# Norm scalings on the activation engine, earlier norm weights, modulation tiles in four column groups, urgent level products: one change to a two-layer backbone kernel

## The chip, the cores and the metric

One core of one Trainium2 chip runs the kernel. The metric is the device time of one execution in microseconds (us), the median of three runs. The core has five engines with a queue each, which run beside each other and wait for each other by semaphores: PE (TensorE: matmuls, and PEld, its weight loads), DVE (VectorE), ACT (ScalarE), POOL (GpSimd) and SP (SyncE, which issues most of the DMAs). An engine works its queue in order.

## The reference, cut to what matters

A backbone of two layers on 512 latent tokens and 256 context tokens, width 1024. Each layer takes six modulation vectors from a conditioning vector (one for latents, one for the context), mixes, and runs a convolution FFN. The mixer of layer 0 has four gated linear-attention heads and a chunk MLP; that of layer 1 has multi-head latent attention with six heads and a Fourier mix. The change touches these parts:

```python
# modulation: 6 x 1024 values for the latents and for the context
mod_l = (silu_c @ ada_w[l] + ada_b[l])[:, None, :]
mod_c = (silu_cc @ ada_w[l] + ada_b[l])[None, None, :]
# layer 0: gated linear attention, one head; readout norm
o = rms_norm(o.transpose(0, 2, 1, 3), onorm_w) * silu(g)
# layer 0: chunk MLP, the "gate values" v are normalised per token and group of 128
u = gelu(u_pre)
v = rms_norm(gelu(v_pre).reshape(bsz, n, 128, 4, 128), vnorm_w)
y = u * (einsum('gts,bnsgc->bntgc', ws, v) + bs.T[:, :, None])
# layer 1: queries and keys are normalised per token and head, rotary part apart
q_nope = rms_norm(q[..., :128], qn_w[:128])
q_pe   = rope_2d(rms_norm(q[..., 128:], qn_w[128:]), cos, sin)
k_pe   = rope_2d(rms_norm(p[..., 640:], kn_w[128:]), cos, sin)
scores = softmax(q @ k.T * 192 ** -0.5)
```

## The kernel before, in words

Everything stays in float32; a product of two matrices is made as three matmuls of high and low parts (`mm3`, L505 to L510). For the weights, `split` (L485) makes the high part `wh` with a cast on ACT (L486) and the low part `wl` with a subtraction, `raw - wh`, on POOL for the kinds in `on_pool` (L498 for a whole 128x1024 chunk, L490 in two halves for the kinds in `by_half`, L495 for other forms of the same). A scheduler of the language orders every engine's queue when the program is built; `high_priority(200)` raises the instructions under it, and pools of tiles (name and number of buffers) decide when a tile may be written again. Weight and modulation loads are issued on SP's queue, some small tables on ACT's.

**Modulation** (`ada_group`, L567). Two layers with three groups each, of 16 half tiles of 128x1024. The conditioning vector stands as a stationary operand of 32 columns (`sc_pad`); a half tile is the moving operand of two matmuls of 512 columns (L577), which land in two of the four groups of 32 PSUM partitions; the other half tile of the same k goes to the other two. Generators in the queue `bg["ada"]` are advanced between other matmuls. At the end of a group the sums are copied (`asb`, L585), transposed (L589) and added to the bias (L594). Layer 0's later groups run under the head projections; layer 1's second group fills the gap between its projections and attention, its third runs in attention.

**GLA heads** (`gla`, a generator in `bg["gla"]` that `tick` advances between projection matmuls). For each of seven levels: block matmuls on PE (L827, or L855 from level 5) from Q products in `qk` and K products merged into `scr`; the result is written into `near` under a mask (L848); then DVE multiplies Q by decay factors (L868), K (L870) and the factors themselves (L872), and ACT copies the K products into `scr` (L835) for the next level. Each of L868 and L870 is one 128x768 multiplication. The tail of a head: squares on ACT (L923), a reciprocal root by Newton steps on DVE (`rsqrt`, L460 to L465, eleven tiny instructions), the scaling into `scr` (L930), transposes on PE (L939), and the products that end in the output slot (L940, L943 on ACT, L944 on POOL).

**Chunk MLP** (L977 to L1021). The gate values `vp` (six token chunks, 512 columns in four groups of 128) get a gelu, squares and a rsqrt `mr` of 24 columns. POOL scales `vp` by `mr` in six 128x512 multiplications (L997). Then `drain("gla")` runs what is left of the last head (its tail), and four groups follow, each with a projection, a gelu, matmuls that have `vp` as the stationary operand (L1011) and products.

**Layer 1, before attention.** The query latents `qt` get squares, `rstd`, a scaling (L1450) and are transposed and split into `lt` (`turn_q`, L1456, ACT L1347, DVE L1348). The table `pewb` of norm weights for the rotary part is fetched by a DMA on ACT's queue (L1433), behind it the rope table (L1435). The rotary keys are scaled with it (L1464), rotated (`rope`, L1364 to L1369) and the table itself is scaled (L1470); this block stands ahead of the call that projects the keys (`keys(0, ...)`, with L1611 and L1613 on ACT, L1614 on DVE). Then keys are scaled (L1622, two on DVE and one on POOL), values projected, and `fill` puts modulation matmuls between.

**Queries** (`scale_queries`, L1568). For each of three pairs of heads, DVE scales the rotary part (L1571) and POOL the rest, in two 128x512 multiplications (L1574). Scores (L1730), maxima on DVE (L1733 to L1735), exponentials on ACT (L1738) and transposes (L1749) follow.

## Time and profile before

| what | value |
|---|---|
| median of three runs | 1649.61 us (1648.12 to 1650.98) |
| the profiled execution's own time | 1649.35 us |
| its span, first to last instruction | 1647.6 us |
| PE busy | 1591.9 us, 97% of the span |
| DVE, ACT, POOL busy | 1140.8, 703.4, 649.1 us |
| mean granted TensorE clock | 0.992 |

The span is 1.75 us shorter than the time; what lies around it is the start and end of the launch. A busy share is an average: where PE is idle, the row of the instruction that follows names in square brackets how long its engine stood idle and what ended that. A granted clock of 1.00 is 2.4 GHz, 0.50 is 1.2 GHz.

### The profile page before, as it was taken

The numbers are of one execution on the slowest core, as the hardware profiler recorded it, in microseconds if no ns is written. First come the engines' busy times: TensorE is split into PE (matmuls) and PEld (weight loads), VectorE is DVE, ScalarE is ACT, GpSimd is POOL, SyncE is SP. The second block draws the span as 40 slices with busy tenths as digits, with TensorE's granted clock in tenths as the row PEclk, the third lists the DMA queues.
The fourth block names the chain that finished last, engine by engine and source line by source line (L and its number), as shares of the span: only waits on it lengthen the run. The fifth ranks groups of instructions, "written<-read, shape, count | busy, mean of one in ns | idle before, by whom it ended". The sixth has DMA issues, their size and how long they took to land.

```text
span 1647.6 us, 28314 instructions
## 1 busy us (share of the span) xinstructions
PE 1591.9 (97%) x11206; PEld 1420.5 (86%) x11206; DVE 1140.8 (69%) x2134; ACT 703.4 (43%) x1328; POOL 649.1 (39%) x421
## 2 busy tenths in 40 slices
PE   8999999989999999999999999898899899999998
PEld 7777777678989999999999989676799898999997
DVE  5447675753565666676666775767874799999984
ACT  4323333523444333233332444465665555555551
POOL 1221223344625566565665513331208322323321
PEclk9999999999999999999999999999999999999999
DMA  9453434333412121222212322752105223223222
GB/s 355 159 187 116 142 116 137 120 102 103 130 50 64 61 80 55 74 77 62 80 55 75 90 68 82 250 171 93 52 27 167 90 85 108 103 90 116 103 78 77
DMA packets 53205, 175.11 MB, mean 106 GB/s; under 512 B 5712, under 2 KB 7760, under 8 KB 53072
## 3 DMA queue, kind: packets, MB, share of 16 engines
q1 hardware_dynamic: 51632, 170.66, 31.1%
q10 hardware_dynamic: 1440, 2.64, 0.4%
q8 instruction: 88, 1.44, 0.3%
q14 instruction: 45, 0.37, 0.1%
HBM read 171.18 MB, written 2.10 MB: 105 GB/s over the span
## 4 chain that ended last, share of the span: by engine, by line
PE 79%; DVE 14%; ACT 2%; DMA 2%; issue 2%; POOL 1%; DVEq 0%; SPq 0%; ACTq 0%; POOLq 0%
PE mm L508 17%; PE mm L510 16%; PE mm L509 16%; PE aux L508 7%; PE aux L509 7%; PE aux L510 7%; PE aux L577 2%; DVE qk L870 1%; DVE qk L868 1%; DVE wp L387 1%; PE aux L1143 1%; PE mm L1730 1%; DMA x<-in_xt_dram 1%; DMA raw<-in_w_dram 1%; PE aux L1749 1%
## 5 line engine op out<-in xcount | busy, mean ns | idle before, releaser
L498 POOL TENSOR_TENSOR wl<-raw,wh 128x1024 fp32r<-128x1024 f32 (+5 forms) x100 | 210.2, 2104 | 356.6 <-ACT wh L486 304.5
L486 ACT CAST wh<-raw 128x1024 fp32r<-128x1024 f32 (+5 forms) x155 | 146.5, 947 | 141.0 <-PE mm L509 63.8
L387 POOL TENSOR_TENSOR wp<-sum,wp 128x512 fp32r<-128x512 f32 x80 | 115.9, 1454 | 163.4 <-ACT wp L385 153.9
L508 PE MATMUL mm<-xt,wh 128*128 128x256 f32 (+1 forms) x384 | 135.1, 353 | 0.9 <-ACT xt L648 0.9
L510 PE MATMUL mm<-xt,wl 128*128 128x512 f32 (+1 forms) x384 | 129.4, 338 | 0.0
L509 PE MATMUL mm<-xt,wh 128*128 128x512 f32 (+1 forms) x384 | 129.3, 337 | 0.0
L509 PE MATMUL mm<-slot,wh 128*128 128x512 f32 (+1 forms) x336 | 113.4, 338 | 1.0 <-POOL slot L1253 0.7
L508 PE MATMUL mm<-slot,wh 128*128 128x512 f32 (+1 forms) x336 | 113.5, 339 | 1.0 <-ACT slot L1252 1.0
L510 PE MATMUL mm<-slot,wl 128*128 128x512 f32 (+1 forms) x336 | 113.1, 337 | 0.0
L385 ACT CAST wp<-sum 128x512 fp32r<-128x512 f32 x100 | 60.8, 620 | 122.2 <-PE aux L509 61.5
L1028 DVE SCALAR_TENSOR_TENSOR xl<-mm,mods,xl 128x512 f32<-128x512 f32 (+1 forms) x84 | 58.5, 696 | 70.7 <-PE mm L510 70.2
L495 POOL TENSOR_TENSOR wl<-raw,wh 128x512 fp32r<-128x512 f32 (+2 forms) x50 | 55.7, 1135 | 129.1 <-ACT wh L486 123.6
L387 POOL TENSOR_TENSOR wp<-raw,wp 128x512 fp32r<-128x512 f32 x60 | 80.0, 1341 | 52.3 <-ACT wp L385 52.3
L385 ACT CAST wp<-raw 128x512 fp32r<-128x512 f32 x100 | 62.1, 621 | 78.5 <-DMA raw<-in_w_dram 27.7
L508 PEld LDWEIGHTS mm<-xt,wh 128*128 128x128 f32 x384 | 72.0, 188 | 27.0 <-issue 16.8
L508 PE MATMUL mm<-kt,wp 128*128 128x256 f32 x320 | 90.4, 282 | 3.8 <-ACT t L1216 3.8
L490 POOL TENSOR_TENSOR wl<-raw,wh 128x512 fp32r<-128x512 f32 x22 | 35.7, 1622 | 138.0 <-DVE t L1245 92.3
L510 PE MATMUL mm<-kt,wp 128*128 128x256 f32 x320 | 89.8, 281 | 0.0
L509 PE MATMUL mm<-kt,wp 128*128 128x256 f32 x320 | 89.7, 280 | 0.0
L510 PEld LDWEIGHTS mm<-xt,wl 128*128 128x128 f32 x384 | 72.3, 188 | 8.2
L509 PEld LDWEIGHTS mm<-xt,wh 128*128 128x128 f32 x384 | 72.2, 188 | 8.3
L509 PE MATMUL mm<-lt,wh 128*128 128x256 f32 (+2 forms) x236 | 78.1, 331 | 1.2 <-DVE lt L1253 1.2
(390 smaller groups left out, 5272.7 us busy)
## 6 DMA issues: line engine op xcount, KB each, us to landing
raw<-in_w_dram SPq DMA_DIRECT2D x162, 512.0 KB, 3.5
ada_t<-in_ada_dram SPq DMA_DIRECT2D x80, 512.0 KB, 4.4
raw<-in_w_dram SPq DMA_DIRECT2D x31, 384.0 KB, 3.1
wp<-in_w_dram SPq DMA_DIRECT2D x20, 512.0 KB, 4.4
kt<-in_ada_dram SPq DMA_DIRECT2D x16, 512.0 KB, 7.0
raw<-in_w_dram SPq DMA_DIRECT2D x10, 256.0 KB, 2.6
xl<-in_xt_dram SPq DMA_DIRECT2D x2, 1024.0 KB, 8.0
out_dram<-xl SPq DMA_DIRECT2D x8, 256.0 KB, 2.0
```

The source lines that it names most:

```text
L385: S.copy(h, a)
L387: e.tensor_tensor(l, a, h.bitcast(F32), op=ALU.subtract)
L486: S.copy(h, raw)
L490: e.tensor_tensor(l[:, c], raw[:, c], h[:, c].bitcast(F32), op=ALU.subtract)
L495: G.tensor_tensor(l[:, c], raw[:, c], h[:, c].bitcast(F32), op=ALU.subtract)
L498: e.tensor_tensor(l, raw, h.bitcast(F32), op=ALU.subtract)
L508: T.matmul(ps, a[0], b[0], start=first, stop=False, **kw)
L509: T.matmul(ps, a[0], b[1], start=False, stop=False, **kw)
L510: T.matmul(ps, a[1], b[0], start=False, stop=last, **kw)
L577: T.matmul(ps[32 * q:32 * q + 32, :], sc_pad[:, k, :], t[:, j * 512:(j + 1) * 512], start=(k == 0), stop=(k == KD - 1))
L868: V.tensor_tensor(qa, qa, pick(FF[:], NT + m, [[2 * m, nb], [-(NT + m), 2], [0, m]]), op=ALU.mult)
L1028: V.scalar_tensor_tensor(xs, ps, gate, xs, op0=ALU.mult, op1=ALU.add)
```

## The change

Seven edits, with the lines of the kernel before. (1) `split`: for the kinds of layer 0 that begin with `ev_` the subtraction on POOL is made as two halves of 512 columns. (2) `ada_group`: a half tile of 1024 columns is the moving operand of four matmuls of 256 columns, one for each group of 32 PSUM partitions, where it was two of 512; the order in which the results are read is changed to match. (3) The two level products L868 and L870 stand under `high_priority(200)`. (4) The last head is run up to its tail before the groups of the chunk MLP, and the tail is run after the first group's projection is issued. (5) The gate values are scaled on ACT, one 128x128 activation for each chunk and group (24 in all, six ahead of each group's projection), where POOL had six multiplications. (6) The table `pewb` lies in a pool that is open from the start; its DMA is written where layer 0's pools close, and since nothing holds it back the scheduler puts it on ACT's queue among the squares of the first norm; the scaling and rotation of the rotary keys moves into `rotate_keys()`, called after the values' projection. (7) `scale_queries`: eight 128x128 activations on ACT for each pair, where POOL had two 128x512 multiplications.

```diff
@@ split
-        if kind[:5] == "down1":
+        if kind[:5] == "down1" or kind[:3] == "ev_" and kind in on_pool:
             n = raw.shape[-1] // 2
-            for e, c in ((G, slice(0, n)), (V, slice(n, 2 * n))):
+            for e, c in ((G, slice(0, n)), (V if kind[:2] == "do" else G, slice(n, 2 * n))):
                 e.tensor_tensor(l[:, c], raw[:, c], h[:, c].bitcast(F32), op=ALU.subtract)
@@ ada_group
-                for j in range(2):
-                    q = 2 * hf + j
-                    T.matmul(ps[32 * q:32 * q + 32, :], sc_pad[:, k, :], t[:, j * 512:(j + 1) * 512],
-                             start=(k == 0), stop=(k == KD - 1))
+                for q in range(4):
+                    T.matmul(ps[32 * q:32 * q + 32, hf * 256:(hf + 1) * 256], sc_pad[:, k, :],
+                             t[:, q * 256:(q + 1) * 256], start=k + hf == 0, stop=k + hf == KD, skip_group_check=True)
@@ gla
             qa = pick(QQ, 0, dd)
-            V.tensor_tensor(qa, qa, ...)
+            with tc.high_priority(200):
+                V.tensor_tensor(qa, qa, ...)
             ka = pick(KK, 0, dd)
-            V.tensor_tensor(ka, ka, ...)
+            with tc.high_priority(200):
+                V.tensor_tensor(ka, ka, ...)
...
-        yield
+        yield "tail"
@@ chunk MLP
-    for c in range(6):
-        a = vp[c // 3][:, c % 3, :].rearrange("p (g d) -> p g d", g=4)
-        G.tensor_tensor(a, a, mr[:, c * 4:c * 4 + 4].unsqueeze(2).to_broadcast([P, 4, P]), op=ALU.mult)
-    drain("gla")
+    while next(bg["gla"][0]) != "tail":
+        pass
     for g in range(4):
+        for c in range(6):
+            a = vp[c // 3][:, c % 3, g * P:(g + 1) * P]
+            S.activation(a, a, AF.Copy, scale=mr[:, c * 4 + g:c * 4 + g + 1])
         ps = proj(("ev_in", 20 + g), X)
+        drain("gla")
@@ layer 1
     l0.close()
     lp = ctx.enter_context(tc.tile_pool(name="l1", bufs=17))
+    pewb = sm.tile([P, 128], F32, tag="pew", name="pewb", bufs=1)
+    nc.scalar.dma_start(pewb[:], pew.to_broadcast([P, 128]))
...
-    pewb = l1c.tile([P, 128], F32, name="pewb")
-    nc.scalar.dma_start(pewb[:], pew.to_broadcast([P, 128]))
...
+    def rotate_keys():
...
     project_v(0)
+    rotate_keys()
     fill(2)
@@ scale_queries
-        q4 = rq.rearrange("p j (g d) -> p j g d", g=2)
-        for j in (slice(0, 2), slice(2, 4)):
-            G.tensor_tensor(q4[:, j], q4[:, j], r[:, j, 0:2].unsqueeze(3).to_broadcast([P, 2, 2, P]), op=ALU.mult)
+        for j in range(4):
+            for g in range(2):
+                q = rq[:, j, g * P:(g + 1) * P]
+                S.activation(q, q, AF.Copy, scale=r[:, j, g:g + 1])
```

Three places where the order of an engine's queue changes:

POOL's queue around the chunk MLP, before and after. In it `wl` is the low part of a weight, `vp` the gate values, `mr` their reciprocal root, `slot` the output of a head (L944; L946 in the change).

```order
L498 TENSOR_TENSOR wl<-raw,wh 128x1024 x9
L997 TENSOR_TENSOR vp<-vp,mr 128x512 x6
L944 TENSOR_TENSOR slot<-slot 128x512
L944 TENSOR_TENSOR slot<-slot 128x256
L498 TENSOR_TENSOR wl<-raw,wh 128x1024
```

```order
L490 TENSOR_TENSOR wl<-raw,wh 128x512 x18
L946 TENSOR_TENSOR slot<-slot 128x512
L946 TENSOR_TENSOR slot<-slot 128x256
L490 TENSOR_TENSOR wl<-raw,wh 128x512 x2
L1025 TENSOR_TENSOR slot<-U,slot 128x512
```

The six multiplications are gone, and POOL has nothing between the last weight and the head's output. On ACT the scalings stand behind the squares of the last head (L925 in the change, L923 before):

```order
L925 ACTIVATE junk,ss<-aux 128x128 x6
L1002 ACTIVATE vp<-vp,mr 128x128 x6
L584 COPY asb<-aux 128x512
L1002 ACTIVATE vp<-vp,mr 128x128 x8
L945 CAST slot<-slot 128x512
L945 CAST slot<-slot 128x256
L1002 ACTIVATE vp<-vp,mr 128x128 x8
L1009 ACTIVATE U<-mm 128x512
L1009 ACTIVATE U<-mm 128x256
L486 CAST wh<-raw 128x1024
L1002 ACTIVATE vp<-vp,mr 128x128 x2
```

So six of the 24 stand ahead of the copy `asb`, and eight ahead of the casts of the head's output.

DVE's queue in the levels of a GLA head, before and after (two levels and the start of a third). L870 is the product of K, L868 that of Q (L872 and L869 in the change, where L872 of before is L874).

```order
L870 TENSOR_TENSOR qk<-qk,slot 128x384x2
L848 COPY_PREDICATED near<-mk,aux 128x192
L868 TENSOR_TENSOR qk<-qk,slot 128x384x2
L872 TENSOR_TENSOR slot<-slot 128x768
L870 TENSOR_TENSOR qk<-qk,slot 128x192x2x2
L848 COPY_PREDICATED near<-mk,aux 128x192
L868 TENSOR_TENSOR qk<-qk,slot 128x192x2x2
L872 TENSOR_TENSOR slot<-slot 128x384
L960 TENSOR_TENSOR slot<-mm,slot 128x512
L960 TENSOR_TENSOR slot<-mm,slot 128x256
L870 TENSOR_TENSOR qk<-qk,slot 128x96x2x4
```

```order
L872 TENSOR_TENSOR qk<-qk,slot 128x384x2
L869 TENSOR_TENSOR qk<-qk,slot 128x384x2
L848 COPY_PREDICATED near<-mk,aux 128x192
L874 TENSOR_TENSOR slot<-slot 128x768
L872 TENSOR_TENSOR qk<-qk,slot 128x192x2x2
L869 TENSOR_TENSOR qk<-qk,slot 128x192x2x2
L848 COPY_PREDICATED near<-mk,aux 128x192
L874 TENSOR_TENSOR slot<-slot 128x384
L962 TENSOR_TENSOR slot<-mm,slot 128x512
L872 TENSOR_TENSOR qk<-qk,slot 128x96x2x4
```

The Q product now follows the K product at once, and the masked copy and the second half of the projection's product stand behind.

DVE's queue in layer 1 where the rotary keys are scaled, before and after; `pewb` is the fetched table, `qt` the query latents, L1348 the low part of the transposed latents that the query projection waits for (in the change L1470 is L1464 of before, L1454 is L1450, L1629 is L1622, L1354 is L1348).

```order
L460 TENSOR_SCALAR rsd<-qs 128x4
L1464 SCALAR_TENSOR_TENSOR kp_9915<-lt,rsd,pewb 128x64
L461 TENSOR_SCALAR rsd<-rsd 128x4
L1464 SCALAR_TENSOR_TENSOR kp_9915<-lt,rsd,pewb 128x64
...
L1470 TENSOR_TENSOR rope_t<-rope_t,pewb 128x512
L465 SCALAR_TENSOR_TENSOR rsd<-rst,rsd 128x4
L1614 TENSOR_REDUCE s_9931<-sq 128x4
L1450 TENSOR_SCALAR qt<-qt,rsd 128x384 x4
...
L1348 SCALAR_TENSOR_TENSOR lt<-aux,vt,lt 128x512
...
L1622 TENSOR_TENSOR lt<-lt,r_9933 128x512 x2
```

```order
L1454 TENSOR_SCALAR qt<-qt,rsd 128x384 x4
L1621 TENSOR_REDUCE s_10078<-sq 128x4 x2
L1350 TENSOR_TENSOR kt<-mm,kt 128x256
L1571 TENSOR_SCALAR s_10078<-s_10078 128x12
L1470 SCALAR_TENSOR_TENSOR kp_10227<-lt,rsd,pewb 128x64
...
L1370 TENSOR_TENSOR lt<-kp_10227,rope_t 128x4x64
L1629 TENSOR_TENSOR lt<-lt,r_10080 128x512 x2
L1375 TENSOR_TENSOR lt<-lt,rope 128x4x2x16 x2
L1476 TENSOR_TENSOR rope_t<-rope_t,pewb 128x512
L1354 SCALAR_TENSOR_TENSOR lt<-aux,vt,lt 128x512 x3
```

The chain of the query latents no longer stands behind the table, but the low parts L1354 (L1348 before) now stand behind the scaled keys and the rotation.

## Rows read from the trace of the kernel before

**Rows 1.** The page's first part: each engine's busy us, share of the span and instructions.

```profile
PE 1591.9 (97%) x11206; PEld 1420.5 (86%) x11206; DVE 1140.8 (69%) x2134; ACT 703.4 (43%) x1328; POOL 649.1 (39%) x421
```

**Rows 2.** Stretches of the span. Columns: the stretch and its length in us; each engine's busy us with the number of instructions; granted clock; share of DMA; GB/s.

```profile
344.28:347.69 3.41, 2.77 (x12) 2.67 (x13) 2.39 (x8) 0.83 (x2) 0.13 (x1) 0.50 0.00 1
1044.01:1047.43 3.42, 3.39 (x16) 2.83 (x20) 3.42 (x8) 2.54 (x7) 1.99 (x2) 0.50 0.02 6
1119.10:1200.00 80.90, 73.72 (x497) 59.98 (x490) 66.90 (x197) 48.88 (x127) 13.34 (x12) 1.00 0.21 72
```

**Rows 3.** The timeline at the last head's tail and the chunk MLP's scaling, DVE, POOL, ACT and PE. Columns: start and duration in us, engine, line, operation, out<-in, shape, count; in brackets the engine's idle time before it and what ended it.

```profile
336.83 0.62 ACT L585 COPY asb<-aux 128x512 f32<-128x512 f32 x1
...
337.01 0.17 DVE L926 TENSOR_SCALAR ss<-ss 128x6 f32<-128x6 f32 x1
337.10 6.03 POOL L997 TENSOR_TENSOR vp<-vp,mr 128x512 f32<-128x512 f32 x6 [2.50 <-DVE mr L465]
...
337.21 0.95 DVE L460 TENSOR_SCALAR rr<-ss 128x6 int32<-128x6 int32 x1
...
342.18 0.96 DVE L463 TENSOR_TENSOR rst<-ss,rr 128x6 f32<-128x6 f32 x1
343.18 0.17 DVE L464 SCALAR_TENSOR_TENSOR rst<-rst,rr 128x6 f32<-128x6 f32 x1
...
344.18 1.02 DVE L930 TENSOR_TENSOR scr<-aux,rr 128x512 f32<-128x512 f32 x2
...
344.92 1.54 PE L939 MATMUL aux<-ct,scr 128*128 128x128 f32 x6 [4.96 <-DVE scr L930]
```

**Rows 4.** Groups of ACT's instructions by line and form: busy us, mean ns of one | idle time before them.

```profile
L1347 ACT ACTIVATE lt<-aux,vt 128x128 fp32r<-128x128 f32 x24 | 8.1, 368 | 5.4 <-PE aux L1590 4.2 <-PE aux L577 0.6 <-DVE lt L1348 0.6
...
L923 ACT ACTIVATE junk<-aux 128x128 f32<-128x128 f32 x24 | 6.3, 278 | 15.1 <-PE aux L918 15.1
```

**Rows 5.** Groups of POOL's instructions by line and form, as in Rows 4.

```profile
L498 POOL TENSOR_TENSOR wl<-raw,wh 128x1024 fp32r<-128x1024 f32 x56 | 135.3, 2416 | 290.2 <-ACT wh L486 273.0 <-PE aux L855 14.3 <-PE aux L827 2.8
...
L495 POOL TENSOR_TENSOR wl<-raw,wh 128x512 fp32r<-128x512 f32 x32 | 41.0, 1303 | 59.7 <-ACT wh L486 57.7 <-issue 1.7 <-DMA raw<-in_w_dram 0.3
```

**Rows 6.** The timeline of two levels of a GLA head, columns as in Rows 3.

```profile
123.49 2.39 POOL L498 TENSOR_TENSOR wl<-raw,wh 128x1024 fp32r<-128x1024 f32 x1 [9.56 <-ACT wh L486]
123.61 3.08 DVE L870 TENSOR_TENSOR qk<-qk,slot 128x768 f32<-128x768 f32 x1
...
126.61 0.36 DVE L848 COPY_PREDICATED near<-mk,aux 128x192 f32<-128x192 uint8 x1
...
126.88 0.94 DVE L868 TENSOR_TENSOR qk<-qk,slot 128x768 f32<-128x768 f32 x1
...
127.97 0.60 PE L827 MATMUL aux<-qk,scr 128*32 128x32 f32 x47 [1.52 <-DVE qk L868]
```

**Rows 7.** L827's matmuls as a group over the whole span: busy us, mean ns of one | PE's idle time before them, and what ended it.

```profile
L827 PE MATMUL aux<-qk,scr 128*32 128x32 f32 x960 | 12.9, 202 | 7.4 <-DVE qk L868 5.2 <-ACT scr L835 2.2
```

**Rows 8.** The timeline of PE, a burst of modulation matmuls that holds both half tiles of a pair (layer 0).

```profile
100.18 1.07 PE L577 MATMUL aux<-ada_t,sc_pad 128*32 128x512 f32 x8
```

**Rows 9.** The same in layer 1, first a burst of three half tiles, then one half tile alone.

```profile
1072.85 1.91 PE L577 MATMUL aux<-kt,sc_pad 128*32 128x512 f32 x12
...
1075.17 1.05 PE L577 MATMUL aux<-kt,sc_pad 128*32 128x512 f32 x4
```

**Rows 10.** L577 alone in stretches: busy us of PE and of PEld (records; two for each instruction), granted clock, share of DMA, GB/s.

```profile
120.00:130.00 10.00, 2.10 (x8) 0.32 (x8) 1.00 0.36 111
208.00:214.00 6.00, 2.10 (x8) 0.29 (x8) 1.00 0.29 87
1052.50:1077.00 24.50, 10.34 (x48) 1.55 (x48) 1.00 0.72 263
1117.00:1175.00 58.00, 9.36 (x40) 1.35 (x40) 0.98 0.29 100
```

**Rows 11.** L577's weight loads: duration in ns, min/median/max, and the starts of the first and the last.

```profile
L577 PEld LDWEIGHTS aux<-ada_t,sc_pad x256: 106/109/154, 70.2 to 1173.0; 128*32 128x32 f32 x128
```

**Rows 12.** The 48 records of a level's block matmuls (L827) on PE.

```profile
122.54 0.63 PE L827 MATMUL aux<-qk,scr 128*32 128x32 f32 x48
```

**Rows 13.** The timeline in layer 1 from the arrival of the table to the query projection, columns as in Rows 3.

```profile
1039.76 0.28 DVE L1464 SCALAR_TENSOR_TENSOR kp<-lt,rsd,pewb 128x64 f32<-128x64 f32 x1 [4.22 <-DMA pewb<-in_pew_dram]
...
1044.04 0.58 PE L508 MATMUL mm<-wh,lt 128*128 128x256 f32 x1 [3.70 <-ACT sq L1613]
...
1045.53 2.15 DVE L1450 TENSOR_SCALAR qt<-qt,rsd 128x384 f32<-128x384 f32 x4
...
1051.43 0.75 DVE L1348 SCALAR_TENSOR_TENSOR lt<-aux,vt,lt 128x512 fp32r<-128x512 f32 x1
...
1052.23 0.44 PE L510 MATMUL mm<-wh,lt 128*128 128x384 f32 x1 [0.22 <-DVE lt L1348]
...
1054.18 2.14 DVE L1622 TENSOR_TENSOR lt<-lt,r 128x512 f32<-128x512 f32 x2
```

**Rows 14.** The timeline in attention, columns as in Rows 3.

```profile
1164.61 0.47 ACT L1738 ACTIVATE pr<-mm,mx 128x256 f32<-128x256 f32 x1 [1.15 <-DVE mx L1735]
...
1165.22 0.39 PE L508 MATMUL mm<-kt,lt 128*128 128x256 f32 x1 [1.12 <-ACT pr L1738]
...
1167.01 2.49 POOL L1574 TENSOR_TENSOR lt<-lt,r 128x512 f32<-128x512 f32 x2 [3.68 <-DVE mx L1740]
```

More of the change, by code (lines that the diff above doesn't have):

```diff
@@ L589, in ada_group @@
             T.transpose(pt[:, b * P:(b + 1) * P], asb[:, b * P:(b + 1) * P], ident)
-        o = mods[l][:, g * 16:(g + 1) * 16, :].rearrange("p (j b) c -> p b j c", b=4)
+        o = mods[l][:, g * 16:(g + 1) * 16, :].rearrange("p (f j e) c -> p f e j c", f=2, e=2)
         i0 = pt[:].rearrange("p (b j r) -> p b j r", b=4, r=32)[:, :, :, 0:2]
-        i1 = vcol("ada_b", l * 48 + g * 16, 16).rearrange("p (j b) -> p b j", b=4).unsqueeze(3)
+        i1 = vcol("ada_b", l * 48 + g * 16, 16).rearrange("p (f j e) -> p f e j", f=2, e=2).unsqueeze(4)
         for b in range(4):
-            V.tensor_tensor(o[:, b], i0[:, b], i1[:, b].to_broadcast([P, 4, 2]), op=ALU.add)
+            f, e = divmod(b, 2)
+            V.tensor_tensor(o[:, f, e], i0[:, b], i1[:, f, e].to_broadcast([P, 4, 2]), op=ALU.add)
         yield
@@ L867, in gla @@
             qa = pick(QQ, 0, dd)
-            V.tensor_tensor(qa, qa, pick(FF[:], NT + m, [[2 * m, nb], [-(NT + m), 2], [0, m]]), op=ALU.mult)
+            with tc.high_priority(200):
+                V.tensor_tensor(qa, qa, pick(FF[:], NT + m, [[2 * m, nb], [-(NT + m), 2], [0, m]]), op=ALU.mult)
             ka = pick(KK, 0, dd)
-            V.tensor_tensor(ka, ka, pick(FF[:], m, [[2 * m, nb], [NT - m, 2], [0, m]]), op=ALU.mult)
+            with tc.high_priority(200):
+                V.tensor_tensor(ka, ka, pick(FF[:], m, [[2 * m, nb], [NT - m, 2], [0, m]]), op=ALU.mult)
             ta = pick(FF[:], 0, [[NT, 2], [2 * m, nb]])
@@ L1460, in backbone @@
     kpe = kt()
-    kp0 = tp.tile([P, 6, 64], F32, tag="t2k", name="kp0")
     kp2 = lt(F32)[:].rearrange("p a b -> p (a b)")[:, 0:768].rearrange("p (c g d) -> p c g d", c=6, g=2)
-    for c in range(6):
-        V.scalar_tensor_tensor(kp0[:, c, :], kvr[c][:, 256:320], kr[:, 6 + c:7 + c], pewb[:, 64:128],
-                               op0=ALU.mult, op1=ALU.mult)
-    G.tensor_copy(kp2[:, 0:2, 0, :], kp0[:, 0:2, :])
-    rope(kp2[:, 2:6, 0, :], kp0[:, 2:6, :])
-    t8 = rope_t[:].rearrange("p (n d) -> p n d", d=64)
-    V.tensor_tensor(t8, t8, pewb[:, 0:64].unsqueeze(1).to_broadcast([P, 8, 64]), op=ALU.mult)
-    G.tensor_copy(kp2[:, :, 1, :], kp2[:, :, 0, :])
+    def rotate_keys():
+        kp0 = tp.tile([P, 6, 64], F32, tag="t2k", name="kp0")
+        for c in range(6):
+            V.scalar_tensor_tensor(kp0[:, c, :], kvr[c][:, 256:320], kr[:, 6 + c:7 + c], pewb[:, 64:128],
+                                   op0=ALU.mult, op1=ALU.mult)
+        G.tensor_copy(kp2[:, 0:2, 0, :], kp0[:, 0:2, :])
+        rope(kp2[:, 2:6, 0, :], kp0[:, 2:6, :])
+        t8 = rope_t[:].rearrange("p (n d) -> p n d", d=64)
+        V.tensor_tensor(t8, t8, pewb[:, 0:64].unsqueeze(1).to_broadcast([P, 8, 64]), op=ALU.mult)
+        G.tensor_copy(kp2[:, :, 1, :], kp2[:, :, 0, :])
     A = []
```

## The prediction

> **What bounds the kernel now.** I read the page first. PE is busy for 1591.9 of 1647.6 us [rows 1], so a change that leaves PE's work alone can win at most the 55.7 us in which PE stands idle, and whatever the clock loses after a long idle time. Then I listed PE's idle times by what ended them, and looked up each that this change can reach. The reader is to see three kinds.
>
> First, the last GLA head's tail. PE stands idle 4.96 us before L939, which waits for the scaling L930 on DVE [rows 3]. Ahead of L930 stands the reciprocal root, eleven tiny instructions. While POOL scales the gate values (6.03 us, six instructions), each of DVE's takes 0.95 to 0.96 us, one for one of POOL's; from 343.18, when POOL is done, the same kind takes 0.17. Behind that idle time the granted clock is 0.50, 1.2 GHz, for 3.41 us with 2.77 of them busy on PE [rows 2].
>
> Second, the levels. K's product L870 took 3.08 us where L868 took 0.94, because POOL's 128x1024 subtraction of 2.39 us had begun 0.12 us earlier [rows 6]; PE then waited 1.52 us. All such waits of L827 come to 7.4 us [rows 7].
>
> Third, layer 1. DVE stands 4.22 us for the table `pewb`, and PE 3.70 us behind it, with the clock at 0.50 for 3.42 us after [rows 2, 13].
>
> Where PE does not wait, the modulation matmuls count in full. A burst of a pair of half tiles takes 1.07 us; a half tile alone takes 1.05, as long as two; three take 1.91 [rows 8, 9]. In a pair, four groups of columns run at once, in a single half tile only two.
>
> My sum is made against the profiled execution, 1649.35 us, which is 0.26 below the median of the three runs; I leave that difference aside. About 0.2% (3.3 us) is what a measurement can tell from no change.
>
> **The parts.**
>
> *Gate values to ACT.* POOL has nothing left to do there, so the eleven instructions go at 0.17 with a pitch of 0.20: from 337.21 to 339.4, L930 starts there and its first half is done some 0.6 later, at 340.0, where it now stands done at 344.9. PE's own work lasts to 339.96 (344.92 less 4.96). The idle time falls from 4.96 to some 0.2, and with it goes the half clock, worth half of the 2.77 us: 1.4. Together −6.1. Bounds: −6.4 if nothing is left; −4.5 if the eleven keep 0.3 and the clock still falls for a part. ACT takes 24 instructions of 128x128 at 0.28 to 0.37 us each [rows 4], 6.7 to 8.9 us in all, of which six stand ahead of `asb` (1.7 to 2.2 us, so it ends by 339.7, still ahead of L939). Their cover is ACT's idle time there; if it were gone, the group's vp matmuls would be late.
>
> *Halves on POOL and urgent products.* A half takes about 1.3 us where the whole takes 2.42 [rows 5]. In rows 3 DVE got in exactly one instruction for each of POOL's. By that, L870 waits for the first half only (1.2 less), but L868 behind it waits for the second half; what is left for certain is that L848 (0.36) no longer stands between them [rows 6]. That is −0.37 for each of six waits, and one where K's product starts earlier by a half: −1.0. Sum −3.2. Bounds: −7.4, if every wait goes, and +1.0, if the halves (0.2 us more POOL time each pair) hit products that were free. The value lies nearest to rows 3, which show the alternation.
>
> *Modulation in four groups.* From rows 8 and 9: a pass of 512 columns adds (1.91−1.07)/2 = 0.42 us, and a burst carries 0.23 beside. A pass of 256 adds 0.21, so a half tile alone takes 0.42+0.23 = 0.65 and a pair stays at 1.07. Whole pairs therefore gain nothing; singles gain 0.40. In layer 0 two pairs are split in two bursts each (2.10 us busy each [rows 10]); the first now goes in one burst (−1.0), the second as one and seven instructions (−0.4): −1.4. In layer 1's fill, twelve half tiles take 10.34 us [rows 10]. In the new order they go as five single ones, one burst of three (six passes, 1.49) and one of four (eight passes, 1.91); the first single one falls into a wait (below), so 4 × 0.65 + 1.49 + 1.91 = 6.0. That is −4.3; I take −4.0, bounds −4.5 and −0.5, the last if the half tiles' arrival becomes the bound. In attention 9.36 us [rows 10] become 7.9 by the same count; half of that lies beside other waits, as PE is idle for 7.2 us of the 80.9 after 1119 [rows 2]: −0.7.
>
> The 320 added weight loads cost nothing in this: L827's weights are of the same shape (128 rows, 32 columns, four groups), and 48 of its records with a load each end in 0.63 us [rows 12], so the loads lie beside the running matmuls. The Trainium skill ("TensorE: Matmul & The Clock Gate", Part 3, the mechanism) says that weight loads overlap running matmuls only where the row groups differ, and here all four use all rows. By that rule the loads would stand in the open, and this term would be a loss (the last rival); rows 12 speak against it, in matmuls of 32 columns only.
>
> *Table and rotation.* The wait of 4.22 us goes, and PE's 3.70 with it [rows 13]. But what PE needs next is L510 at 1052.23, which waits for L1348, and L1348 now stands behind two keys' products (2.14), and the rotation. DVE now begins its wait at 1035.54 (1039.76 less 4.22). Without it, ten more instructions of the latents' root at 0.20 and a reduction of some 0.7 bring L1450 to 1038.3, where it now starts at 1045.53: 7.2 earlier. Put between L1450 and L1348 are six products with the table at 0.28, 1.7 together, L1622's 2.14, and the rotation and the scaling of the table, some 2.0 (an estimate, four instructions of the sizes of these rows and a wait for POOL's share): 5.8 later. L1348 thus comes 1.4 earlier. So most of what is won at 1040 is waited out again before 1052, in a new idle time of PE, with perhaps another stretch of half clock. I take −0.7; bounds −3.0 (the added instructions lie in DVE's waits) and +2.5 (the clock falls on busy work). The DMA at the start costs ACT one issue: +0.2.
>
> *Queries to ACT.* POOL's 2.5 us for each pair [rows 14] go. ACT gets 8 × 0.28 to 0.37, 2.2 to 3.0 us, three times; PE waited there 1.12 us on ACT's exponentials, ACT 1.15 on DVE's maxima. I take 0; bounds −1.5 (DVE's freed time) and +4.
>
> Sum: −6.1 −3.2 −1.4 −4.0 −0.7 −0.7 +0.2 = −15.9, so 1649.35 − 15.9 = **1633.5 us**.
>
> **The rivals.**
>
> *The waits move* (0.26). Halves win nothing, as products alternate with the halves, and the fill's winnings are waited out on DVE or on arriving tiles. What stays is the tail (−6.1), layer 0's splits (−1.4) and a bit of the rest (−0.7): 1641.2. For it speaks that DVE is 69% busy [rows 1] and that the low parts now stand behind the keys; against it, that behind 1052 the rows show PE running without a wait on DVE.
>
> *More than forecast* (0.12). All of L827's waits go (−7.4), the table's term is −3.0 and attention gains 2.2 in all: −6.1−7.4−1.4−4.0−3.0−2.2 = −24.1, 1625.3. For it: priority lets the products pass the projection's; against it: rows 3.
>
> *ACT becomes attention's bound* (0.06). Three times 2.2 to 3.0 us stand in front of exponentials that PE waits for, 7.8, and the tail's −6.1 and −1.4 are all else that holds: 1649.6, no change. Against it: ACT is 43% busy [rows 1], and pair 0's lie ahead of attention.
>
> *Weight loads in the open* (0.04), slower. 320 more at 0.109 us [rows 11] are 34.9 us, less the tail, the levels and the table (10.0): 1674. It decides from a burst of a pair of more than 1.07 + 10.0/40 = 1.32 us. The rule of the Trainium skill named above would bring this about; L827's rows are against it.
>
> **How the numbers follow.** Forecast 0.52, the others as given. Faster by over 0.2%: forecast and the first two rivals, 0.90. Within 0.2%: the third, 0.06. Slower: 0.04. The range goes down to 1624.0, past the second rival's value by the 1.4 us by which attention's and layer 0's terms are uncertain, and up to 1644.0, past the first's by 2.8, about what the queries' bound of +4 leaves beside −1.2 of the rest. Left out are the last two rivals (0.10) and as much of the others' edges.
>
> **What would show it.** Right: L460 to L465 at 337 all near 0.17, no idle time of over 1 us before L939, no 0.50 behind it; half tiles alone in 0.65; no wait on `pewb`; an idle time on PE before the query projection that L1348 ends. Wrong: products of levels still at 2.5 us with PE waiting as long; pair bursts over 1.3; PE waits on exponentials that stand behind the query scalings.

## The result and the profile after

The changed kernel takes 1635.2 us, the median of four runs (1633.43 to 1638.72), where the kernel before took 1650.3 beside it (1648.12 to 1653.59): a ratio of 0.991 [0.9886, 0.9933]. The profiled execution took 1633.43 us with a span of 1631.6, so 15.9 us less than the profiled one of before. PE's idle time fell from 55.7 to 47.0 us (span less busy) and its busy time by 7.3. The first part of the page after, columns as in [rows 1]:

```profile
PE 1584.6 (97%) x11526; PEld 1429.8 (88%) x11526; DVE 1128.5 (69%) x2134; ACT 717.2 (44%) x1376; POOL 653.9 (40%) x457
```

Where the time came from shows when the start of the same PE instruction is taken in both traces and subtracted. Worked out so, in us:

| stretch, by the time in before | after less before at its end | gained or lost in it | forecast |
|---|---|---|---|
| start, to 70 | +0.25 | +0.25 | +0.2 |
| levels and layer 0's splits, to 316 | −7.5 | −7.75 | −4.6 |
| tail, to 387 | −14.3 | −6.8 | −6.1 |
| behind layer 0's FFN norm, to 466 | −12.4 | +1.9 | none |
| to the fill, about 1025 | −12.7 | −0.3 | none |
| fill and table, to 1084 | −14.3 | −1.6 | −4.7 |
| attention, to 1287 | −13.2 | +1.1 | −0.7 |
| behind the last norm, to 1292 | −15.1 | −1.9 | none |
| to the end | −16.0 | −0.9 | none |

So the total is as forecast, and four of its terms are not. Each difference is that of one execution against one: at 70, executions of kernels with the same edit 6 stood between 2.0 us earlier and 2.9 us later than before, so the +0.25 of the first line alone says nothing, and only what comes on top within a stretch is read below.

**The tail went as forecast.** The timeline after, columns as in [rows 3]:

```profile
329.56 1.87 ACT L1002 ACTIVATE vp<-vp,mr 128x128 f32<-128x128 f32 x6 [0.22 <-DVE mr L465]
329.64 0.17 DVE L460 TENSOR_SCALAR rr<-ss 128x6 int32<-128x6 int32 x1
...
331.66 0.17 DVE L465 SCALAR_TENSOR_TENSOR rr<-rst,rr 128x6 f32<-128x6 f32 x1
...
331.87 1.02 DVE L932 TENSOR_TENSOR scr<-aux,rr 128x512 f32<-128x512 f32 x2
...
332.61 0.88 PE L941 MATMUL aux<-ct,scr 128*128 128x128 f32 x6 [0.28 <-DVE scr L932]
```

From the root's first instruction to its last, 2.2 us now stand where [rows 3] have 7.1, each at 0.17. PE's idle time is 0.28 instead of 4.96. Windows after, columns as in [rows 2]; the text comes back to the later ones:

```profile
332.00:345.00 13.00, 12.72 (x83) 11.23 (x82) 6.43 (x13) 8.73 (x25) 7.13 (x6) 1.00 0.38 138
448.00:456.00 8.00, 6.53 (x33) 5.83 (x34) 6.89 (x19) 3.38 (x8) 0.00 (x0) 0.79 0.00 0
...
1040.65:1044.50 3.85, 3.85 (x24) 2.19 (x23) 1.21 (x5) 0.77 (x2) 0.00 (x0) 0.57 0.42 142
...
1102.50:1106.50 4.00, 4.00 (x23) 1.92 (x15) 2.70 (x12) 0.42 (x1) 0.00 (x0) 0.57 0.01 4
1275.50:1283.00 7.50, 7.50 (x61) 7.13 (x60) 5.08 (x13) 3.72 (x9) 0.06 (x1) 1.00 0.01 2
```

The first line is the tail: granted clock 1.00, where [rows 2] have 0.50.

**The levels gained more than forecast.** L827 as a group after, which answers to [rows 7]:

```profile
L827 PE MATMUL aux<-qk,scr 128*32 128x32 f32 x960 | 12.9, 202 | 2.8 <-DVE qk L869 1.6 <-ACT scr L835 1.0
```

Its waits fell by 4.6 us. The deepest levels' matmuls, L855, had a wait of their own that the forecast did not count. In before:

```profile
L855 PE MATMUL aux<-qk,scr 128*128 128x128 f32 x96 | 12.2, 276 | 1.2 <-DVE qk L868 1.2
```

It is 0.0 after. Together that is 5.8 of some 6.3 us (7.75 less the splits' 1.4); some 0.7 of the gain lies ahead of the first level, between 70 and 114. Two levels after, columns as in [rows 6]:

```profile
122.49 0.95 DVE L872 TENSOR_TENSOR qk<-qk,slot 128x768 f32<-128x768 f32 x1
122.83 4.16 POOL L490 TENSOR_TENSOR wl<-raw,wh 128x512 fp32r<-128x512 f32 x2 [9.14 <-PE aux L827]
123.36 0.95 DVE L869 TENSOR_TENSOR qk<-qk,slot 128x768 f32<-128x768 f32 x1
124.97 0.60 PE L827 MATMUL aux<-qk,scr 128*32 128x32 f32 x46
...
292.05 3.25 POOL L490 TENSOR_TENSOR wl<-raw,wh 128x512 fp32r<-128x512 f32 x2 [1.77 <-ACT wh L486]
292.27 1.88 DVE L872 TENSOR_TENSOR qk<-qk,slot 128x768 f32<-128x768 f32 x1
...
294.07 2.04 DVE L869 TENSOR_TENSOR qk<-qk,slot 128x768 f32<-128x768 f32 x1
...
296.26 0.62 PE L827 MATMUL aux<-qk,scr 128*32 128x32 f32 x48 [1.41 <-DVE qk L869]
```

The second pair is what was forecast: each product stands behind one half (1.88 and 2.04), and PE waits 1.41. The first pair is what was not: both products keep their 0.95, and it is POOL that is late (two halves in 4.16 instead of some 2.6). PE does not wait.

**The half tiles have the forecast durations.** A whole pair, 16 records in layer 0, and one half tile alone, 8 records in layer 1, which answer to [rows 8] and [rows 9]; and L576 (L577 before) alone in windows, which answer to [rows 10]:

```profile
99.90 1.07 PE L576 MATMUL aux<-ada_t,sc_pad 128*32 128x256 f32 x16
...
1050.48 0.64 PE L576 MATMUL aux<-kt,sc_pad 128*32 128x256 f32 x8
```

```profile
120.00:130.00 10.00, 1.08 (x16) 0.51 (x16) 1.00 0.27 88
205.00:211.00 6.00, 1.68 (x16) 0.54 (x16) 1.00 0.35 116
1036.00:1062.00 26.00, 5.80 (x80) 2.13 (x80) 0.93 0.49 176
1100.00:1160.00 60.00, 8.86 (x80) 2.51 (x80) 0.97 0.26 89
```

The added weight loads lie beside the running matmuls: the pair of 16 takes 1.07 us as the pair of 8 did, so PE has paid nothing for them. Attention's ten half tiles (the last line) take 8.86 us where the forecast had 7.9.

**Layer 1 has another wait instead.** The timeline after, columns as in [rows 13]:

```profile
1035.74 2.12 DVE L1629 TENSOR_TENSOR lt<-lt,r 128x512 f32<-128x512 f32 x2
...
1038.19 0.68 DVE L1476 TENSOR_TENSOR rope_t<-rope_t,pewb 128x512 f32<-128x512 f32 x1
...
1038.79 2.06 DVE L1354 SCALAR_TENSOR_TENSOR lt<-aux,vt,lt 128x512 fp32r<-128x512 f32 x3
...
1039.58 0.44 PE L510 MATMUL mm<-wh,lt 128*128 128x384 f32 x1 [3.24 <-DVE lt L1354]
```

PE's 3.70 on the table is gone, and 3.24 behind the low parts L1354 stands in its place, with a granted clock of 0.57 behind it (the window at 1040.65). The difference stood at −12.7 us where the fill begins and at −18.2 at 1049 of before; L510 starts at 1039.58 instead of 1052.23, which is −12.65. So the 5.5 us won by then were waited out there, and what the stretch keeps is won behind it. Ahead of L510 stand two of the fill's twelve half tiles (at 1033.03 and 1035.15); the other ten stand behind it.

**Attention lost.** The timeline at the first scores, columns as in [rows 14]:

```profile
1097.65 2.45 ACT L1581 ACTIVATE lt<-lt,r 128x128 f32<-128x128 f32 x8 [2.66 <-DVE r L465]
...
1100.48 0.46 ACT L1746 ACTIVATE pr<-mm,mx 128x256 f32<-128x256 f32 x1
...
1101.08 0.38 PE L508 MATMUL mm<-kt,lt 128*128 128x256 f32 x1 [2.74 <-ACT pr L1746]
```

PE waits 2.74 us for an exponential that stands behind the eight new scalings, and then runs at 0.57 (the window at 1102.5).

### The profile page after: what moved, and what is told of

It is laid out like the page before. It is cut to its first block, busy times and chain, and to the rows that moved or that the text cites. A ratio compares the mean times of both kernels' runs of the same rounds, so it can differ in the third digit from the quotient of the medians.

```text
span 1631.6 us, 29062 instructions
## 1 busy us (share of the span) xinstructions
PE 1584.6 (97%) x11526; PEld 1429.8 (88%) x11526; DVE 1128.5 (69%) x2134; ACT 717.2 (44%) x1376; POOL 653.9 (40%) x457
## 3 DMA queue, kind: packets, MB, share of 16 engines
q10 hardware_dynamic: 1440, 2.64, 0.4%
## 4 chain that ended last, share of the span: by engine, by line
PE 81%; DVE 12%; ACT 3%; issue 2%; DMA 1%; POOL 1%; SPq 0%; ACTq 0%; DVEq 0%; POOLq 0%
PE mm L508 17%; PE mm L510 17%; PE mm L509 17%; PE aux L508 7%; PE aux L509 7%; PE aux L510 7%; PE aux L576 2%; DVE wp L387 1%; PE aux L1147 1%; DVE qk L872 1%; DVE qk L869 1%; PE mm L1738 1%; DMA raw<-in_w_dram 1%; PE aux L855 1%; PE aux L1757 1%
## 5 line engine op out<-in xcount | busy, mean ns | idle before, releaser
L490 POOL TENSOR_TENSOR wl<-raw,wh 128x512 fp32r<-128x512 f32 x118 | 171.1, 1468 | 367.4 <-ACT wh L486 203.5
L498 POOL TENSOR_TENSOR wl<-raw,wh 128x768 fp32r<-128x768 f32 (+6 forms) x52 | 94.2, 1813 | 115.3 <-ACT wh L486 87.7
L509 PE MATMUL mm<-xt,wh 128*128 128x512 f32 (+1 forms) x384 | 130.0, 339 | 0.0
L510 PE MATMUL mm<-xt,wl 128*128 128x512 f32 (+1 forms) x384 | 129.7, 338 | 0.0
L509 PE MATMUL mm<-slot,wh 128*128 128x512 f32 (+1 forms) x336 | 113.4, 337 | 0.7 <-POOL slot L1257 0.7
L510 PE MATMUL mm<-slot,wl 128*128 128x512 f32 (+1 forms) x336 | 113.3, 338 | 0.0
L510 PE MATMUL mm<-kt,wp 128*128 128x256 f32 x320 | 89.8, 280 | 0.0
L509 PE MATMUL mm<-kt,wp 128*128 128x256 f32 x320 | 89.7, 280 | 0.0
L509 PEld LDWEIGHTS mm<-xt,wh 128*128 128x128 f32 x384 | 72.8, 190 | 8.2
L510 PEld LDWEIGHTS mm<-xt,wl 128*128 128x128 f32 x384 | 72.8, 190 | 8.1
L509 PE MATMUL mm<-lt,wh 128*128 128x256 f32 (+2 forms) x236 | 78.5, 333 | 1.2 <-DVE lt L1257 1.2
```

What stands on the lines that cost most here:

```text
L490: e.tensor_tensor(l[:, c], raw[:, c], h[:, c].bitcast(F32), op=ALU.subtract)
L498: e.tensor_tensor(l, raw, h.bitcast(F32), op=ALU.subtract)
L509: T.matmul(ps, a[0], b[1], start=False, stop=False, **kw)
L510: T.matmul(ps, a[1], b[0], start=False, stop=last, **kw)
```

## The experiments

Theory A: the tail, the levels and the table gain as their waits fall; the fill's gain is waited out behind L1354, and the queries on ACT cost attention some 3 us. Its rivals, one for each run: that the tail's gain came from another edit; that halves, not urgency, carry the levels; that the four groups gained in place; and that the queries' cost lies elsewhere.

### The tail by itself

**Edits 4 and 5 put into the kernel before.**

```diff
-        yield
+        yield "tail"
...
-    for c in range(6):
...
-        G.tensor_tensor(a, a, mr[...], op=ALU.mult)
-    drain("gla")
+    while next(bg["gla"][0]) != "tail":
+        pass
     for g in range(4):
+        for c in range(6):
...
+            S.activation(a, a, AF.Copy, scale=mr[...])
         ps = proj(("ev_in", 20 + g), X)
+        drain("gla")
```

> The kernel before with only the gate values moved: 24 activations on ACT, the last head run up to its tail first. Theory (POOL's six multiplications slow DVE's eleven tiny instructions, one for one): these go at 0.17 us, the idle time of 4.96 us before the head's last transposes goes and the half clock behind it with it, 6 us at the end of the tail and at the end: 1644. Rival (the tail waits for the statistics or for ACT, and the earlier run of the tail is what counts): the tiny instructions stay near 0.95 us, or the idle time moves to another wait; less than 3 us.

Measured: 1642.32 us, 0.9951 [0.9937, 0.9964]. The timeline at the tail, columns as in [rows 3]:

```profile
338.23 0.17 DVE L460 TENSOR_SCALAR rr<-ss 128x6 int32<-128x6 int32 x1
...
341.18 0.87 PE L939 MATMUL aux<-ct,scr 128*128 128x128 f32 x6 [0.21 <-DVE scr L930]
```

The root's instructions take 0.17 and PE waits 0.21. By the trace it gains 6.0 us between 338 and 387, and 5.4 are left at the end; by the medians it is 7.8 (5.9 to 10.4), and the profiled execution was the slowest of its five. So the tail's term is shown by itself, and it is the largest of the forecast. What edit 4 gives without edit 5 no run shows.

### The levels: halves or urgency

**Whole chunks on POOL again**, the products still urgent:

```diff
-        if kind[:5] == "down1" or kind[:3] == "ev_" and kind in on_pool:
+        if kind[:5] == "down1":
```

> The changed kernel with POOL subtracting whole 128x1024 chunks again for the mixer of layer 0; the level products stay urgent. By the end of the levels (at 308 in the changed kernel) PE stood 7.5 us earlier than before the change, 1.4 of it modulation bursts. Theory A (halves let DVE in after 1.3 us): products of 2.5 to 3.1 us come back, PE's waits before the block matmuls come to 4 us or more, and the end of the levels is 2.5 to 4 us later: 1638. Theory B (urgency alone carries it, since the masked copy and the projection's products no longer stand in front): less than 1 us later: 1635 to 1636.

Measured: 1638.41 us, 0.9931 [0.9918, 0.9943]. **Halves kept, the products not urgent:**

```diff
-            with tc.high_priority(200):
-                V.tensor_tensor(qa, qa, ...)
+            V.tensor_tensor(qa, qa, ...)
...
-            with tc.high_priority(200):
-                V.tensor_tensor(ka, ka, ...)
+            V.tensor_tensor(ka, ka, ...)
```

> The changed kernel without the raised priority of the two level products; POOL keeps the halves. Theory A (halves): products wait for half chunks only, the end of the levels is 1 to 2 us later than in the changed kernel: 1636. Theory B (urgency): PE's waits before the block matmuls come back, 4 to 6 us by the end of the levels: 1640.

Measured: 1642.36 us, 0.9952 [0.9938, 0.9966]. L827 as a group, with whole chunks:

```profile
L827 PE MATMUL aux<-qk,scr 128*32 128x32 f32 x960 | 13.0, 202 | 4.0 <-DVE qk L869 2.2 <-ACT scr L835 1.7
```

and without the urgency:

```profile
L827 PE MATMUL aux<-qk,scr 128*32 128x32 f32 x960 | 12.9, 202 | 7.0 <-DVE qk L868 4.8 <-ACT scr L835 2.2
```

Against 2.8 with both, L827 waits 4.0 and 7.0; L855 waits 0.6 and 0.0. By the trace, from 70 to the end of the heads, whole chunks cost 3.1 us (0.8 of it ahead of the first level) and the lost urgency 4.6, each with the other edit in place. Halves alone thus leave L827 nearly where it was (7.0 of 7.4), as the first rival said of them, though they take L855's wait away (1.2 to 0.0); urgency carries the larger part.

### The fill: two groups or four

**Edit 2 undone**, all else as changed (the order in which the results are read goes back with it):

```diff
-                for q in range(4):
-                    T.matmul(ps[32 * q:32 * q + 32, hf * 256:(hf + 1) * 256], ..., t[:, q * 256:(q + 1) * 256], ...)
+                for j in range(2):
+                    q = 2 * hf + j
+                    T.matmul(ps[32 * q:32 * q + 32, :], ..., t[:, j * 512:(j + 1) * 512], ...)
```

> The changed kernel with the modulation matmuls of before: a half tile feeds two column groups with 512 columns. Theory (whole pairs gain nothing, single half tiles 0.4 us; in layer 1's fill much of that is waited out again behind the query latents and the keys): bursts of one half tile take 1.05 us again, layer 0's levels end 1.0 to 1.4 us later, the fill 1 to 3 us later, in all 2 to 4 us: 1638. Rival 1 (the fill's bursts stood in full on the path): 5 to 6 us, 1641. Rival 2 (weight loads cost what the groups won): 1635 or less.

Measured: 1637.38 us, 0.9928 [0.9914, 0.9942], against 0.991 [0.9886, 0.9933] with four; the intervals overlap. The timeline in layer 1:

```profile
1036.65 2.05 DVE L1354 SCALAR_TENSOR_TENSOR lt<-aux,vt,lt 128x512 fp32r<-128x512 f32 x3
1037.44 0.44 PE L510 MATMUL mm<-wh,lt 128*128 128x384 f32 x1 [2.64 <-DVE lt L1354]
...
1039.06 1.92 PE L577 MATMUL aux<-kt,sc_pad 128*32 128x512 f32 x4
```

A half tile alone takes two groups' time again (1.92 at half clock), yet PE is not later at the end of the fill: it waits 2.64 us on L1354 instead of 3.24, and up to 1072 its clock stands at 0.50 in two stretches (from 1037.80 and 1065.11), where the changed kernel has three (from 1041.16, 1061.64 and 1068.47). From 1025 to 1084 of before it gains 1.3 us by the trace, the changed kernel 1.5. So in this order the four groups win about nothing in the fill. In layer 0 the pair that was in two bursts at 125 goes in one here too: that −1.0 comes from the order, not from the groups.

In attention the four groups do pay: between 1084 and 1287 of before this kernel loses 4.2 us and the changed one 1.1, and ten half tiles take 12.15 us of PE here and 8.86 with four groups:

```profile
1100.00:1160.00 60.00, 12.15 (x40) 1.48 (x38) 0.98 0.26 88
```

**The query latents' low parts ahead of the scaled keys and the rotation:**

```diff
     stats_keys(0)
-    scale_keys(0, *k0)
     project_v(0)
-    rotate_keys()
-    fill(2)
     for k in range(3):
         turn_q(k)
-    fill(2)
+    scale_keys(0, *k0)
+    rotate_keys()
+    fill(4)
```

> The changed kernel with the query latents turned (three transposes each with its low part on DVE) ahead of the scaling of the keys and of the rotation, whose calls come behind. Theory (the low parts waited behind 2.1 us of scaled keys, 0.5 of rotation and 0.7 of table): the idle time of 3.24 us at 1036 falls under 1 us, the half clock behind it goes, PE reaches the query projection 3 to 4 us earlier, and of this 3 us or more are left at the end: about 1631. Rival (PE's next wait is for the modulation tiles, whose loads come at about one in 1.3 us, or for the keys): the idle time comes back as waits on DMA or on the keys' copies before 1070 and the end moves by less than 1 us: 1634 to 1636.

Measured: 1631.29 us, 0.9891 [0.9875, 0.9907].

```profile
1034.07 0.74 DVE L1354 SCALAR_TENSOR_TENSOR lt<-aux,vt,lt 128x512 fp32r<-128x512 f32 x1
1034.87 0.44 PE L510 MATMUL mm<-wh,lt 128*128 128x384 f32 x1 [1.25 <-DVE lt L1354]
```

The wait falls from 3.24 to 1.25, no half-clock stretch follows it, and layer 1 gains 5 to 6 us up to attention by the trace. Of that, some 2 are given back in attention and 2.6 behind the last norm, where PE now stands idle for 2.42 us and the clock falls. By the medians 3.9 us are left, with intervals that overlap. So the place of the keys' work on DVE was the bound of this stretch. Whether the four groups pay once that bound is gone is asked last.

### The table by itself

**Edit 6 put into the kernel before.**

```diff
+    pewb = sm.tile([P, 128], F32, tag="pew", name="pewb", bufs=1)
+    nc.scalar.dma_start(pewb[:], pew.to_broadcast([P, 128]))
...
-    pewb = l1c.tile([P, 128], F32, name="pewb")
-    nc.scalar.dma_start(pewb[:], pew.to_broadcast([P, 128]))
...
+    def rotate_keys():
...
     project_v(0)
+    rotate_keys()
     fill(2)
```

> The kernel before with only the table's earlier fetch and the rotation moved behind the values. Theory (the 3.70 us of PE's idle time come back before the query projection, where the low parts now stand behind the scaled keys and the rotation): PE reaches the query projection 0 to 2 us earlier, the end moves by less than 2 us: 1648 to 1650. Rival (the wait for the table stood in full on the path): 4 us and the half clock, 5 us in all: 1645.

Measured: 1647.77 us, 0.9991 [0.9982, 1.0001]. PE's 3.70 is gone, and the next wait is there:

```profile
1052.90 0.44 PE L510 MATMUL mm<-wh,lt 128*128 128x384 f32 x1 [2.73 <-DVE lt L1350]
```

L510 starts at 1052.90 where it was 1052.23 before; 0.51 of that was there at 1035 already, so up to L510 nothing is won. Behind it the stretch gains all the same: from 1025 to 1084 it is 3.4 us by the trace of this execution, the fastest of its twelve. By the medians it is 2.0, and the −0.7 of the forecast lies in the interval (−3.0 to +0.2 us).

### The queries

**Edit 7 undone**, all else as changed:

```diff
-        for j in range(4):
-            for g in range(2):
...
-                S.activation(q, q, AF.Copy, scale=r[:, j, g:g + 1])
+        q4 = rq.rearrange(...)
+        for j in (slice(0, 2), slice(2, 4)):
+            G.tensor_tensor(q4[:, j], q4[:, j], r[...], op=ALU.mult)
```

> The changed kernel with one edit undone: the queries are scaled by two 128x512 multiplications on POOL again. Theory (the eight activations of pair 1, 2.45 us in a row, stand ahead of the squares and exponentials on ACT, so PE waits 2.74 us at 1098 and then works 3 us at half clock): that idle time falls to about 1 us or less, no half clock behind it, and the time is 3 to 4 us shorter than the changed kernel, about 1631. Rival (that idle time comes from DVE's maxima, whatever engine scales the queries): idle time of 2 us or more stays and the time is within 1 us of 1635. Second rival (POOL's two-operand multiplications hold DVE up there by as much): 1635 to 1637.

Measured: 1629.79 us, 0.9872 [0.9854, 0.9889], by the medians 5.4 us less than the change. By the trace this execution stands 0.9 us later than the changed one at 1055 and 4.2 earlier at 1273, so 5.1 us are won there; 1.1 of it is given back behind the last norm. Half of the 5.1 lies in attention. The timeline at the first scores:

```profile
1095.15 2.55 POOL L1580 TENSOR_TENSOR lt<-lt,r 128x512 f32<-128x512 f32 x2 [2.04 <-DVE r L465]
...
1098.20 0.36 PE L508 MATMUL aux<-kt 128*128 128x256 f32 x1 [2.18 <-DVE mx L1741]
...
1098.96 0.47 ACT L1745 ACTIVATE pr<-mm,mx 128x256 f32<-128x256 f32 x1 [3.92 <-DVE mx L1742]
```

PE's 2.74 is gone, but it now waits 2.18 on DVE's maxima, and the clock falls behind that as well. That the idle time would go was wrong, since a second wait had stood behind the first.

The other half (2.5 us) lies ahead of 1070, at the end of the fill, where theory A had nothing. There stand the scalings of the first pair of heads. In the changed kernel:

```profile
1054.18 2.46 ACT L1581 ACTIVATE lt<-lt,r 128x128 f32<-128x128 f32 x8 [3.79 <-DVE r L465]
...
1058.70 0.92 ACT L486 CAST wh<-raw 128x516 fp32r<-128x516 f32 x2
...
1060.79 0.39 PE L509 MATMUL mm<-wl,lt 128*128 128x258 f32 x1 [0.67 <-POOL wl L498]
```

With the queries on POOL the same weight casts start at 1057.33, and L509 does not wait. The window behind, columns as in [rows 2], in the changed kernel; with the queries on POOL its granted clock is 1.00:

```profile
1060.00:1070.00 10.00, 7.63 (x37) 6.75 (x37) 5.20 (x14) 7.21 (x18) 5.76 (x8) 0.75 0.70 249
```

So the eight scalings also push the casts of the next weights back. A part of the 2.5 us is the clock, which stands at 0.50 twice for 3.4 us there (from 1061.64 and 1068.47) and not at all in the run with the queries on POOL; whether the scalings bring that on each time no run shows.

### What follows for a better kernel

**Both: low parts first and queries on POOL.**

> The changed kernel with both amendments: the query latents turned ahead of the keys' scaling and the rotation, and the queries scaled on POOL. Theory (two waits at different places, each with its own stretch of half clock, so their gains add): the sum of the two alone, 3 to 4 and 4 to 6 us less than the changed kernel: 1626 to 1628. Rival (both gains stand in the same slack ahead of pair 1, so the larger alone is left): 1630.

Measured: 1624.5 us, 0.9841 [0.9825, 0.9858]. **And the maxima urgent:**

```diff
+        with tc.high_priority(200):
             for s in range(2):
                 V.tensor_reduce(m[:, s:s + 1], ps[s], axis=AX.X, op=ALU.max)
```

(so too for the two small instructions that follow them.)

> As the one with both amendments, and the maxima of the scores raised in priority on DVE. Theory (with the queries on POOL, PE waits 2.18 us in pair 1 for the second maximum, which stands behind a sum of squares of the keys): that idle time falls under 1 us and with it the half clock behind it; 2 to 3 us less than with both amendments, 1624 to 1625. Rival (the statistics that are pushed back delay the next pair's keys or queries by as much): within 1 us, with new waits on the keys' low parts.

Measured: 1621.74 us, 0.9825 [0.981, 0.984], the fastest of all, some 13 us below the change. The wait of about 2 us on the maxima is gone; the 2.8 us between the two medians lie within overlapping intervals. **The same with two groups**, edit 2 undone in it:

> The kernel with both amendments and urgent maxima, with the modulation matmuls of before (two column groups of 512). In the changed kernel itself, going back to two groups left PE no later at the end of layer 1's fill, since the wait for the query latents' low parts took up what shorter bursts won. Theory (that wait hid it): with the wait down to 1.3 us, two groups cost more, 2 to 4 us by the end of the fill (1060) beside 0.4 in layer 0, and 3 to 5 us in all: 1625 to 1627. Rival (the fill's bursts are hidden by other waits, the tiles' landing or the keys' low parts): within 1 us at 1060 and within 2 us at the end: 1622 to 1624.

Measured: 1626.41 us, 0.9861 [0.9843, 0.9879]. The modulation matmuls alone in the fill, columns as in [rows 10], with four groups and with two:

```profile
1030.00:1061.00 31.00, 8.00 (x124) 2.95 (x116) 1.00 0.78 287
```

```profile
1030.00:1066.00 36.00, 10.81 (x64) 2.03 (x64) 1.00 0.77 277
```

Here the clock is 1.00 in both and PE pays for the single half tiles: 124 records are 15.5 half tiles and 64 are 16. By the trace the two-group kernel stands 2.4 us later at 1030 already; on top of that come 2.9 us to 1060 and some 7 to the end, 3.3 of them in attention. By the medians it is 4.7 (1626.41 − 1621.74), with intervals that only just part. So the fill's term was not false of PE's work; in the changed kernel it was waited out, and it comes back once L1354 is early and the queries are off ACT.

## Why the prediction was right in sum and wrong in parts

- **Tail (−6.1): right.** It measured −6.0 at 350 and −6.8 at 387, and alone −6.0. The mechanism is shown: without POOL's scaling DVE's eleven instructions take 0.17.
- **Levels (−3.2): right in direction, mis-sized; about −6.3.** The step that failed is "L868 behind it waits for the second half". Urgency issues both products so early that in some levels POOL is the one that waits, as at 122.49. And the sum counted L827's waits only; L855's 1.2 fell to nothing too, and some 0.7 came ahead of the levels.
- **Layer 0's splits (−1.4): right**, 2.10 to 1.08 and 2.10 to 1.68, though the first comes from the order alone.
- **Fill (−4.0) and table (−0.7): together −1.6; the fill's term failed.** The bursts' durations were right to 0.01 (1.07, and 0.64 for 0.65), and the twelve half tiles go in the bursts that were forecast. What failed is that their winnings were booked as if nothing else in the stretch would move. What the two half tiles ahead of L510 win is waited out there, although the same text found that L1354's chain sets when that projection starts and said of the table's wait that "most of what is won at 1040 is waited out"; here the first rival was right. And behind L510 the queries on ACT take 2.5 us that stood at 0. Put side by side, the stretch from 1025 to 1084 gains 3.4 us with the table alone, 4.2 with the four groups added and the queries on POOL, and 1.5 as changed (single executions). So of what it kept, most was the table's, and the four groups' share was some 0.2 to 0.8. Terms that end in one wait have to be summed before that wait is applied.
- **Attention (−0.7) and queries (0): wrong in sum, +1.1 in the trace, and both mis-sized.** The four groups win some 3 us there, by both pairs of kernels that differ in them alone (+4.2 to +1.1, and 3.3 of the 7), where the forecast took 0.7 from the bursts of the order before. The queries cost 5.1 us by the trace and 5.4 by the medians, past the bound of +4, half of it in attention. There the exponential of the next scores stood behind the eight scalings, as the third rival had it, though for one pair of the three; the first pair's scalings, which that rival set aside as "ahead of attention", delayed weight casts instead.
- **Not foreseen: the stretches of half clock** that come and go elsewhere with the moved times. Behind layer 0's FFN norm one came (the window at 448, 0.79: +1.9 by the table above), two came at the end of the fill (from 1061.64 and 1068.47), and behind the last norm one went (−1.9). In before, the window behind the last norm and the row it follows:

```profile
1288.00:1295.50 7.50, 6.66 (x36) 6.46 (x37) 6.25 (x16) 3.38 (x8) 0.00 (x0) 0.65 0.00 0
```

```profile
1286.56 1.19 PE L636 MATMUL aux<-ct,ny 128*128 128x128 f32 x4 [2.48 <-DVE ny L465]
```

and the same matmuls after, with the clock at 1.00 in the window at 1275.5:

```profile
1273.40 0.68 PE L636 MATMUL aux<-ct,ny 128*128 128x128 f32 x4 [1.81 <-DVE ny L465]
```

- **Weight loads in the open (rival, 0.04): refuted** by the pair's 1.07 us with 16 loads, far from its 1.32. The Trainium skill ("TensorE: Matmul & The Clock Gate", Part 3, the mechanism) has weight loads overlap running matmuls only where the row groups differ; this trace does not agree, since here all four groups use all rows and the burst did not grow. The same section also lets a load go ahead into a background weight buffer, which would fit the trace; no run here tells the two apart.

That the errors cancel is luck: the levels gained 3.1 us more than forecast, the fill with the table 3.1 less and attention 1.8 less, and inside these last two the queries' cost took about what the table and attention's half tiles won beyond their terms. A forecast of the total at 0.991 alone would not have shown it; the differences by stretch do.

One question stays partly open: why the levels' two products pass POOL's subtraction at 122 and alternate with it at 292. The order on DVE is the same in both. The rows show who had begun first: at 122 K's product, 0.34 us ahead of POOL's first half (122.49 and 122.83), at 292 that half, 0.22 ahead of the product (292.05 and 292.27), and in both the later one waited. Why at 122 the second product went ahead of the waiting half as well, they do not show; no run here moved that alone.

## What to carry to other kernels

A wait that is removed is worth what the next wait behind it leaves: name the instruction that the slowest engine needs next, and count everything that now stands ahead of it, since a single call's place (the keys' scaling ahead of the query latents' low parts) took back the 5.5 us that had been won ahead of it. Where two engines take turns, as DVE and POOL do here, moving long work away from tiny instructions on a critical chain, and giving the products that release the slowest engine priority, paid more than cutting the long work in halves. And a term that "costs nothing" on an engine 44% busy has to be checked at the one instruction that is waited for, not by the share.
